# A transformer block on one core: half of the cross attention's output projection as a wide product, x^T scaled by ScalarE, finer first loads

## The chip, the core and the metric

The kernel runs on 1 core of a Trainium2 chip. The metric is the device time of one execution in microseconds; lower is better. The engines are called by their names or as the profile abbreviates them: TensorE (PE, its weight loads PEld), VectorE (DVE), ScalarE (ACT), GpSimd (POOL) and SyncE (SP), which issues most of the DMAs.

## What is computed

One layer of an encoder, batch 1, 256 tokens of 2048 features, all in f32, with weights from memory:

```
h  = rms_norm(x, g_mix);  proj = h @ w_in
x  = x + concat(MLA(proj), DiffAttention(proj)) @ w_out
hx, hm = rms_norm(x, g_xattn), rms_norm(mem, g_mem)
xq, xk, xv = hx @ w_xq, hm @ w_xk, hm @ w_xv          # 4 heads of 128, 256 memory tokens
xo = softmax(xq . xk / sqrt(128)) @ xv                 # 256 x 512
x  = x + xo @ w_xo                                     # 512 -> 2048
hf = rms_norm(x, g_ffn)
x  = x + (silu(hf @ w_gate) * (hf @ w_up)) @ w_down
out = rms_norm(x, g_final)
```

## The kernel before, in words

**Precision.** TensorE multiplies in a reduced f32 format, so each operand is split into a high part and a low part (names ending in `h` and `l`: `wh`, `wl` for weights, `x2T_h`, `x2T_l` for activations), and each product is three matmuls: high by high, high by low, low by high (`mm`, L99 to L101). The split (`split_into`) is a cast to the high part on ScalarE (L107) and a subtraction for the low part on VectorE (L108). Every weight that comes from memory goes through both engines once before TensorE can read it.

**Tiles.** The 256 tokens are two token tiles of 128 (`tt`). An output block is 128 tokens by 512 columns in one bank of PSUM. A K tile is 128 rows of the contraction. `project` runs over the K tiles of a 512-column block, with one accumulator for each token tile: 6 matmuls for a K tile.

**Wide products.** `wide_project` computes 1024 columns at once for both token tiles, over pairs of K tiles, so a pair is a 2 x 2 block product. A plain pair ("P") takes 8 block products, 24 matmuls. A summed pair ("W") computes the same with 7 block products, 21 matmuls, from sums and differences of blocks. Its activations need eight forms of 128 x 128 (`summed_pair`, L236 to L252): where they come from PSUM, ScalarE copies one block (`a21`, L244), VectorE makes four differences, each from the one before (L245 to L248), and then `split_into` makes high and low parts of the first four blocks and the four differences. Its weights need four sums on VectorE and their splits. The four products that are shared by two outputs stand in banks `q1`, `q5`, `q7`, `q6`, which are added into the residual stream `x_res` at the end (`leave`). Two groups of four PSUM banks change roles after each wide product (`banks.reverse()`).

**Order of work.** A scheduler places the instructions on each engine by simulated times, from the program text and the tile pools (24 buffers of activations, 3 of raw weights, 4 each of `wh` and `wl`). The loads of weights stay in program order on SP's queue. A buffer that isn't free, or an engine's order, is what an instruction waits for.

**The start.** The first projection (`w_in_lat`, 16 K tiles of 832 columns, 512 for the queries' and 320 for the keys' latents) begins as the first loads land. The x^T tiles (128 x 256 a K tile) are scaled by the gains (`gains`) and split in one go (`Transposed.load`): by ScalarE (L113), and for K tile 0 by VectorE (L111). Before, K tiles 0 and 1 are loaded singly, x^T and weights in turn; from K tile 2 on the weights come two K tiles at a time, x^T first two and then four. Two small tables for the positions (`pos`, `invf`) are queued behind the weights of K tiles 4 and 5; GpSimd and ScalarE make the trigonometric tables from them. Until the data are there, TensorE runs 12 matmuls of zeros (`wps`, L386).

**Around the change.** After the cross attention's heads (`heads_out`: value times transposed probabilities, into the bank `po`, two heads each, split into `xoT`), the output projection is four calls of `project` over 4 K tiles of `xoT`, one for each 512 columns. Each result is added to `x_res` by VectorE. Then `column_T` transposes the 512 new columns of a token tile with four TensorE transposes (L504) into a bank `pt`, VectorE multiplies them by the gains of the next norm into `x2T_f`, `split_into` makes `x2T_h` and `x2T_l`, and ScalarE takes the sum of squares (L206, `junk`). The gated feed-forward reads x2T: first a narrow chunk of 512 gate and 512 up columns (`project`, 16 K tiles), and then wide ones, for which `x2T_f` is multiplied by the row scale (`rrow`, L870) and split again as `x2n`.

```
x2T(kt):  K tiles 0-3 from column 0, 4-7 from column 1, 8-11 from column 2, 12-15 from column 3
```

## Time and profile before

| | |
|---|---|
| time, median of 3 runs | 1143.33 us (1143.21 to 1143.75) |
| the profiled execution | 1143.3 us, its span 1141.5 us |
| mean granted TensorE clock | 0.998 of full speed |
| TensorE busy | 1131.6 us, 99% of the span, 5394 matmuls and transposes recorded |
| VectorE busy | 980.6 us, 86% |
| ScalarE busy | 649.7 us, 57% |
| GpSimd busy | 57.6 us, 5% |
| DMA | 222.13 MB, mean 195 GB/s |

The span runs from the first to the last instruction of the profiled execution, and its time has what lies around it, 1.8 us. Times in the profile are counted from the span's start. A matmul's busy time reaches past the start of the next one, since they are pipelined; what a matmul costs is read from start to start.

### The profile page before, as it was taken

What the parts mean: (1) busy time and instruction counts of PE and PEld (TensorE: products, weight loads), DVE (VectorE), ACT (ScalarE), POOL (GpSimd) and SP (SyncE); (2) the same over time, 40 slices, a digit from 0 to 9 for tenths busy, and PEclk for the clock granted to TensorE, in tenths of its full rate; (3) what the DMA queues carried; (4) which work ended last, traced back from release to release, by engine and by line L of the source; (5) the groups of instructions that cost most, each with busy time, mean ns of one, the idle gap of its engine ahead of it and who ended that gap; (6) DMA issues with size and microseconds to landing.
All of it is one profiled execution on the core that took longest, in us unless ns stands there. A gap on an engine that the chain in (4) does not pass through costs nothing.

```text
span 1141.5 us, 14385 instructions
## 1 busy us (share of the span) xinstructions
PE 1131.6 (99%) x5394; PEld 946.4 (83%) x5394; DVE 980.6 (86%) x1341; ACT 649.7 (57%) x930; POOL 57.6 (5%) x75
## 2 busy tenths in 40 slices
PE   9999999999999999999999999999999999999997
PEld 7888888888888888888888888888888888888886
DVE  7688766878997776989899998998999898998975
ACT  6755455556567555665555464564554664654642
POOL 4920000000001000000000000000000000000000
PEclk9999999999999999999999999999999999999999
DMA  9655334536557445455655555555555555565543
GB/s 355 222 204 183 141 113 146 185 135 227 214 204 271 152 162 179 161 212 187 215 192 213 181 198 216 185 195 211 184 204 202 214 192 199 194 238 207 191 169 129
DMA packets 34485, 222.13 MB, mean 195 GB/s; under 512 B 4208, under 2 KB 4976, under 8 KB 10096
## 3 DMA queue, kind: packets, MB, share of 16 engines
q1 hardware_dynamic: 32688, 216.60, 53.3%
q0 software_dynamic: 864, 3.15, 0.8%
q10 hardware_dynamic: 864, 1.47, 0.4%
q8 instruction: 42, 0.69, 0.2%
q14 instruction: 27, 0.22, 0.1%
HBM read 219.11 MB, written 2.10 MB: 194 GB/s over the span
## 4 chain that ended last, share of the span: by engine, by line
PE 98%; DMA 1%; issue 0%; ACT 0%; DVE 0%; SPq 0%; POOLq 0%; POOL 0%; ACTq 0%
PE acc L100 26%; PE acc L99 26%; PE acc L101 26%; PE q L99 4%; PE q L100 4%; PE q L101 4%; PE pt L504 2%; PE ppt L652 1%; DMA wraw<-in_w_in_lat 1%; PE psc L100 1%; PE psc L101 1%; PE psc L99 1%; PE pt L924 0%; PE acckv L99 0%; PE acckv L101 0%
## 5 line engine op out<-in xcount | busy, mean ns | idle before, releaser
L107 ACT CAST wh<-wraw 128x1024 fp32r<-128x1024 f32 (+2 forms) x401 | 389.3, 990 | 331.7 <-PE acc L101 285.5
L108 DVE TENSOR_TENSOR wl<-wraw,wh 128x1024 fp32r<-128x1024 f32 (+2 forms) x401 | 455.3, 1150 | 91.0 <-ACT wh L107 89.6
L107 ACT CAST wh<-tsum 128x1024 fp32r<-128x1024 f32 (+1 forms) x96 | 96.4, 1006 | 52.7 <-PE acc L101 23.1
L100 PE MATMUL acc<-wl,x2n_h 128*128 128x512 f32 x320 | 124.5, 390 | 0.0
L101 PE MATMUL acc<-wh,x2n_l 128*128 128x512 f32 x320 | 123.9, 389 | 0.0
L108 DVE TENSOR_TENSOR wl<-tsum,wh 128x1024 fp32r<-128x1024 f32 (+1 forms) x96 | 111.5, 1163 | 14.1 <-ACT wh L107 14.0
L99 PE MATMUL acc<-wh,x2n_h 128*128 128x512 f32 x320 | 109.7, 390 | 0.0
L100 PE MATMUL acc<-wl,x0T_h 128*128 128x512 f32 x224 | 88.7, 396 | 0.1
L101 PE MATMUL acc<-wh,x0T_l 128*128 128x512 f32 x224 | 88.2, 394 | 0.0
L99 PE MATMUL acc<-wh,x0T_h 128*128 128x512 f32 x224 | 86.8, 395 | 0.7 <-ACT wh L107 0.5
L100 PE MATMUL acc<-wl,hT_h 128*128 128x512 f32 x188 | 73.3, 392 | 0.0
L100 PE MATMUL q<-wl,forms_h 128*128 128x512 f32 x187 | 72.7, 389 | 0.0
L101 PE MATMUL q<-wh,forms_l 128*128 128x512 f32 x187 | 72.6, 389 | 0.0
L101 PE MATMUL acc<-wh,hT_l 128*128 128x512 f32 x188 | 72.4, 389 | 0.0
L101 PEld LDWEIGHTS acc<-wh,x2n_l 128*128 128x128 f32 x320 | 60.1, 188 | 12.4
L100 PEld LDWEIGHTS acc<-wl,x2n_h 128*128 128x128 f32 x320 | 60.1, 188 | 12.3
L99 PEld LDWEIGHTS acc<-wh,x2n_h 128*128 128x128 f32 x320 | 59.9, 188 | 12.3
L99 PE MATMUL q<-wh,forms_h 128*128 128x512 f32 x187 | 65.6, 389 | 0.0
L100 PE MATMUL acc<-wl,forms_h 128*128 128x512 f32 x167 | 64.8, 389 | 0.0
L101 PE MATMUL acc<-wh,forms_l 128*128 128x512 f32 x167 | 64.8, 389 | 0.0
L99 PE MATMUL acc<-wh,hT_h 128*128 128x512 f32 x188 | 64.5, 391 | 0.0
L99 PE MATMUL acc<-wh,forms_h 128*128 128x512 f32 x167 | 62.9, 389 | 0.0
(406 smaller groups left out, 2240.4 us busy)
## 6 DMA issues: line engine op xcount, KB each, us to landing
wraw<-in_w_gate SPq DMA_DIRECT2D x44, 1024.0 KB, 4.8
wraw<-in_w_up SPq DMA_DIRECT2D x44, 1024.0 KB, 4.8
wraw<-in_w_dn SPq DMA_DIRECT2D x41, 1024.0 KB, 4.8
wraw<-in_w_in SPq DMA_DIRECT2D x24, 1024.0 KB, 4.8
wraw<-in_w_out SPq DMA_DIRECT2D x16, 1024.0 KB, 4.9
wraw<-in_w_in_lat SPq DMA_DIRECT2D x7, 832.0 KB, 7.5
wraw<-in_w_xk SPq DMA_DIRECT2D x4, 1024.0 KB, 4.9
wraw<-in_w_xq SPq DMA_DIRECT2D x4, 1024.0 KB, 5.0
```

Source lines behind the costliest of these rows:

```text
L99: nc.tensor.matmul(o, l.h, r.h, start=start, stop=False)
L100: nc.tensor.matmul(o, l.h, r.l, start=False, stop=False)
L101: nc.tensor.matmul(o, l.l, r.h, start=False, stop=stop)
L107: last_cast[0] = nc.scalar.copy(out=dst.h, in_=src).ins
L108: last_split[0] = nc.vector.tensor_tensor(out=dst.l, in0=src, in1=dst.h.bitcast(F32), op=ALU.subtract).ins
L504: nc.tensor.transpose(out=pt[:, j * P:(j + 1) * P], in_=src[:, j * P:(j + 1) * P], identity=ident)
L652: nc.tensor.transpose(out=pt[:, kt * S + tt * P:kt * S + (tt + 1) * P], in_=p[:, tt, kt * P:(kt + 1) * P], identity=ident)
```

## The change

It has four parts. **(1)** The first 1024 columns of the cross attention's output become one `wide_add` over two pairs of K tiles: the first pair (heads 0 and 1) is summed, the second plain. `heads_out` makes the summed pair's forms straight from the bank `po`, so these heads exist as forms only, and the remaining two `project` calls take their K tiles from the pair's first forms. As the summed pair is the first to write three of the accumulators, the start flags are taken from `used`. **(2)** In `transposed`, the gain is applied to the x2T columns by four ScalarE passes, one for each 128 columns, with the gain as the scale of the pass. **(3)** K tiles 0 to 5 of the start are loaded singly, x^T and weights in turn, and x^T comes two K tiles at a time from there on. **(4)** The warm-up has three matmuls of 256 columns in place of four. The host packs `w_xo` to match.

```diff
+XO_KINDS = "WP"
...
             mm(Q[1], A11, b11[:, 0, :], *own)
-            mm(accs[0][1], S3, b11[:, 1, :], False, stop)
+            mm(accs[0][1], S3, b11[:, 1, :], not used[0][1], stop)
             mm(Q[5], S5, t1, *own)
             mm(Q[7], S7, t3, *own)
-            mm(accs[0][0], A12, b21[:, 0, :], False, stop)
+            mm(accs[0][0], A12, b21[:, 0, :], not used[0][0], stop)
             mm(Q[6], S6, t2, *own)
-            mm(accs[1][0], A22, t4, False, stop)
+            mm(accs[1][0], A22, t4, not used[1][0], stop)
+            for tt, oc in ((0, 1), (0, 0), (1, 0)):
+                used[tt][oc] = True
...
-    for n in [512] * 8 + [256] * 4:
+    for n in [512] * 8 + [256] * 3:
         nc.tensor.matmul(wps[:, :n], warm[:, :P], warm[:, :n], start=True, stop=True)
...
-        def load_one(self, k):
-            self.load(0, k, 1)
+        def load_one(self, kt):
+            self.load(kt // 4, kt % 4, 1)
...
     for i in range(8):
-        if i == 1:
-            x0T.load(0, 2, 2)
-        elif i and i % 2 == 0:
-            x0T.load(i // 2)
+        one_by_one = i < 3
+        if not one_by_one:
+            x0T.load(i // 2, i % 2 * 2, 2)
...
-        for k, w in enumerate(weights(a["w_in_lat"][i], i == 0, before_k=x0T.load_one if i == 0 else None,
+        for k, w in enumerate(weights(a["w_in_lat"][i], one_by_one,
+                                      before_k=lambda k: one_by_one and x0T.load_one(2 * i + k),
                                       cut=QL if i == 0 else None, raw=lat_raw if i == 0 else None)):
...
-    def transposed(dst, src, tt, n, gain=None, raw=None):
+    def transposed(dst, src, tt, n, gain=None, raw=None, by_scalar=False):
...
-            nc.vector.tensor_tensor(out=g[:, :n, :], in0=pv, in1=gain.unsqueeze(2).to_broadcast([P, n, P]),
-                                    op=ALU.mult)
+            if by_scalar:
+                for j in range(n):
+                    nc.scalar.activation(g[:, j, :], pv[:, j, :], AF.Copy, scale=gain[:, j:j + 1])
+            else:
+                nc.vector.tensor_tensor(out=g[:, :n, :], in0=pv, in1=gain.unsqueeze(2).to_broadcast([P, n, P]),
+                                        op=ALU.mult)
...
-        split_into(dst, po.rearrange("p (j t) -> p j t", j=2))
+        po = po.rearrange("p (j t) -> p j t", j=2)
+        if dst is None:
+            return summed_pair(po[:, :, :P], po[:, :, P:], True)
+        split_into(dst, po)
+        return Pair(dst)
...
-        transposed(t, xs, tt, 4, gain[:, 4 * oc:4 * oc + 4], raw)
+        transposed(t, xs, tt, 4, gain[:, 4 * oc:4 * oc + 4], raw, raw is not None)
...
-    xoT = act_tile(name="xoT")
-    for half in range(2):
-        heads_out(xoT[:, 2 * half:2 * half + 2, :], [pxT[half][:, 0:2, :], pxT[half][:, 2:4, :]], xv, 2 * half)
+    xoT = act_tile(name="xoT")[:, 0:2, :]
+    xo = [heads_out([None, xoT][half], [pxT[half][:, 0:2, :], pxT[half][:, 2:4, :]], xv, 2 * half)
+          for half in range(2)]
...
+    wide_add(xo, a["w_xo2"], (0, 1), XO_KINDS, 0)
     for oc in range(4):
-        accs = project(lambda kt: xoT[:, kt, :], [a["w_xo"][oc, 0]])
+        if oc >= 2:
+            add_out(project(lambda kt: tuple(xo[kt // 2].at(kt % 2, tt) for tt in range(NT)), [a["w_xo"][oc - 2, 0]]), oc)
         x2p.append(act_tile(name="x2T"))
         x2raw.append(act.tile([P, 4, S], F32, name="x2T_f", tag="act"))
         for tt in range(NT):
-            xs = x_res[tt][:, oc * 512:(oc + 1) * 512]
-            nc.vector.tensor_tensor(out=xs, in0=xs, in1=accs[tt], op=ALU.add)
             column_T(x2p[oc], oc, tt, g_f, x2ss, x2raw[oc])
```

The change adds two or more lines above every line of the program, so L99 to L101 become L101 to L103, L107 and L108 become L109 and L110, L206 becomes L208, L504 becomes L508, L870 becomes L882; the ScalarE passes with the gain are L514. Numbers behind a name are the tile's.

TensorE, from the last value product of the second half of the heads into the output projection; before:

```order
L101 MATMUL po_4071<-pxT_h_3808,val_l_4049 128x256
L99 MATMUL po_4071<-pxT_h_3808,val_h_4048 128x256
L100 MATMUL po_4071<-pxT_l_3809,val_h_4048 128x256
L101 MATMUL po_4071<-pxT_h_3808,val_l_4049 128x256
L99 MATMUL acc_4087<-wh_4091,xoT_h_4054 128x512
L100 MATMUL acc_4087<-wl_4092,xoT_h_4054 128x512
L99 MATMUL acc_4088<-wh_4091,xoT_h_4054 128x512
L100 MATMUL acc_4088<-wl_4092,xoT_h_4054 128x512
```

and with the change:

```order
L103 MATMUL po_4095<-pxT_h_3819,val_l_4060 128x256
L101 MATMUL po_4095<-pxT_h_3819,val_h_4059 128x256
L102 MATMUL po_4095<-pxT_l_3820,val_h_4059 128x256
L103 MATMUL po_4095<-pxT_h_3819,val_l_4060 128x256
L101 MATMUL q1_4117<-wh_4121,forms_h_4080 128x512
L102 MATMUL q1_4117<-wl_4122,forms_h_4080 128x512
L103 MATMUL q1_4117<-wh_4121,forms_l_4081 128x512
L101 MATMUL acc_4112<-wh_4121,forms_h_4080 128x512
L102 MATMUL acc_4112<-wl_4122,forms_h_4080 128x512
L101 MATMUL q5_4118<-wh_4134,forms_h_4080 128x512
L102 MATMUL q5_4118<-wl_4135,forms_h_4080 128x512
L101 MATMUL acc_4111<-wh_4125,forms_h_4080 128x512
```

The last four rows before the projection are the same. Before, its first matmul reads the high part of heads 0 and 1 (xoT_h), which takes one cast; now it reads the first pair's forms, and the seven matmuls behind it read them too.

TensorE, from the end of the last output projection to the gate, with the change (pt_4239 is token tile 1 of column 0, pt_4255 and pt_4268 are column 1, pt_4322 and pt_4335 column 2, pt_4389 and pt_4402 column 3; acc_4427 and acc_4428 are the gate's accumulators for the two token tiles):

```order
L103 MATMUL acc_4349<-wh_4356,xoT_l_4066 128x512
L508 MATMUL pt_4239<-ident_104,xres1_112 128x128 x4
L508 MATMUL pt_4255<-ident_104,xres0_111 128x128 x4
L508 MATMUL pt_4268<-ident_104,xres1_112 128x128 x4
L508 MATMUL pt_4322<-ident_104,xres0_111 128x128 x4
L101 MATMUL acc_4427<-wh_4431,x2T_h_4223 128x512
L102 MATMUL acc_4427<-wl_4432,x2T_h_4223 128x512
L103 MATMUL acc_4427<-wh_4431,x2T_l_4224 128x512
L101 MATMUL acc_4427<-wh_4431,x2T_h_4223 128x512
L102 MATMUL acc_4427<-wl_4432,x2T_h_4223 128x512
L103 MATMUL acc_4427<-wh_4431,x2T_l_4224 128x512
L101 MATMUL acc_4427<-wh_4435,x2T_h_4223 128x512
```

and a little further, behind pt_4335's four transposes and five more gate matmuls:

```order
L508 MATMUL pt_4389<-ident_104,xres0_111 128x128 x4
L508 MATMUL pt_4402<-ident_104,xres1_112 128x128 x4
L101 MATMUL acc_4428<-wh_4431,x2T_h_4223 128x512
L102 MATMUL acc_4428<-wl_4432,x2T_h_4223 128x512
L101 MATMUL acc_4427<-wh_4465,x2T_h_4252 128x512
```

The transposes of column 0's second token tile now stand behind the whole last product, and twelve more of them, twelve gate matmuls and another twelve transposes stand between them and the first matmul of acc_4428.

ScalarE in the same place; before:

```order
L206 ACTIVATE junk_4196,x2ss_4086<-xres0_112 128x512
L206 ACTIVATE junk_4207,x2ss_4086<-xres1_113 128x512
L107 CAST x2T_h_4123<-x2T_f_4125 128x4x128
L107 CAST wh_4347<-wraw_4345 128x1024
L107 CAST x2T_h_4123<-x2T_f_4125 128x4x128
L107 CAST x2T_h_4184<-x2T_f_4186 128x4x128
L107 CAST wh_4351<-wraw_4345 128x1024
L107 CAST x2T_h_4184<-x2T_f_4186 128x4x128
L206 ACTIVATE junk_4257,x2ss_4086<-xres0_112 128x512
L107 CAST wh_4381<-wraw_4379 128x1024
```

and with the change:

```order
L109 CAST wh_4431<-wraw_4429 128x1024
L109 CAST wh_4435<-wraw_4429 128x1024
L208 ACTIVATE junk_4346,x2ss_4110<-xres1_112 128x512
L514 ACTIVATE x2T_f_4225<-pt_4239,gains_101 128x128 x4
L514 ACTIVATE x2T_f_4254<-pt_4255,gains_101 128x128 x4
L514 ACTIVATE x2T_f_4254<-pt_4268,gains_101 128x128 x4
L208 ACTIVATE junk_4400,x2ss_4110<-xres0_111 128x512
L109 CAST wh_4465<-wraw_4463 128x1024
L109 CAST wh_4469<-wraw_4463 128x1024
L109 CAST x2T_h_4223<-x2T_f_4225 128x4x128
L109 CAST x2T_h_4252<-x2T_f_4254 128x4x128 x2
```

Before, the casts of column 0's two token tiles (x2T_h_4123) stand with one weight cast between them. Now the first one's stands further ahead, and between the second one's transposes (pt_4239) and its cast (x2T_h_4223) stand twelve scaled passes, two sums of squares and two weight casts.

VectorE, at the end of the narrow gate's weights and the row scale; before:

```order
L108 TENSOR_TENSOR wl_4454<-wraw_4447,wh_4453 128x1024
L108 TENSOR_TENSOR wl_4553<-wraw_4550,wh_4552 128x1024
L108 TENSOR_TENSOR wl_4557<-wraw_4550,wh_4556 128x1024
L108 TENSOR_TENSOR wl_4587<-wraw_4584,wh_4586 128x1024
L108 TENSOR_TENSOR wl_4591<-wraw_4584,wh_4590 128x1024
L870 TENSOR_TENSOR x2T_f_4125<-x2T_f_4125,rrow_4487 128x1024
L870 TENSOR_TENSOR x2T_f_4186<-x2T_f_4186,rrow_4487 128x1024
L870 TENSOR_TENSOR x2T_f_4247<-x2T_f_4247,rrow_4487 128x1024
L870 TENSOR_TENSOR x2T_f_4308<-x2T_f_4308,rrow_4487 128x1024
L108 TENSOR_TENSOR wl_4621<-wraw_4618,wh_4620 128x1024
```

and with the change:

```order
L110 TENSOR_TENSOR wl_4534<-wraw_4531,wh_4533 128x1024
L110 TENSOR_TENSOR x2T_l_4387<-x2T_f_4388,x2T_h_4386 128x4x128 x2
L110 TENSOR_TENSOR wl_4538<-wraw_4531,wh_4537 128x1024
L882 TENSOR_TENSOR x2T_f_4225<-x2T_f_4225,rrow_4571 128x1024
L882 TENSOR_TENSOR x2T_f_4254<-x2T_f_4254,rrow_4571 128x1024
L882 TENSOR_TENSOR x2T_f_4321<-x2T_f_4321,rrow_4571 128x1024
L882 TENSOR_TENSOR x2T_f_4388<-x2T_f_4388,rrow_4571 128x1024
L110 TENSOR_TENSOR wl_4637<-wraw_4634,wh_4636 128x1024
L110 TENSOR_TENSOR wl_4641<-wraw_4634,wh_4640 128x1024
```

The four multiplications by the row scale stood behind the splits of four weight tiles of the up product (wl_4553 to wl_4591); now they stand ahead of them.

## Rows read from the trace of the kernel before

**Rows 1.** Page, chain of work that ended last: share of the span by engine.
```profile
PE 98%; DMA 1%; issue 0%; ACT 0%; DVE 0%; SPq 0%; POOLq 0%; POOL 0%; ACTq 0%
```

**Rows 2.** Timeline, 0 to 45 us: start, busy us, what ran [idle before <-releaser].
```profile
4.54 0.35 DVE L111 TENSOR_SCALAR x0T_h<-xraw,gains 128x256 fp32r<-128x256 f32 x1 [3.42 <-DMA gains<-in_gains]
...
10.11 0.31 PE L101 MATMUL acckv<-wh,x0T_l 128*128 128x320 f32 x1
...
10.93 0.50 PE L99 MATMUL acc<-wh,x0T_h 128*128 128x512 f32 x1 [0.51 <-ACT wh L107]
...
11.64 0.31 PE L99 MATMUL acckv<-wh,x0T_h 128*128 128x320 f32 x1
...
11.98 0.50 PE L100 MATMUL acc<-wl,x0T_h 128*128 128x512 f32 x1
```

**Rows 3.** Timeline, ScalarE, 0 to 40 us; and DMA GB/s, one number per us.
```profile
7.22 0.98 ACT L107 CAST wh<-wraw 128x512 fp32r<-128x512 f32 x2 [1.61 <-DMA wraw<-in_w_in_lat]
...
9.99 1.68 ACT L107 CAST wh<-wraw 128x832 fp32r<-128x832 f32 x2 [0.97 <-DMA wraw<-in_w_in_lat]
...
GB/s 0 16 194 370 299 332 383 399 376 419 435 358 144 300 428 409 435 432 399 426 406 461 397 393 417 437 413 436 417 407 430 437 387 148 213 393 418 41 57 221
```

**Rows 4.** Timeline, VectorE from 53 us and TensorE from 56 us.
```profile
53.57 1.05 DVE L520 TENSOR_SCALAR cq<-cq,rq 128x512 f32<-128x512 f32 x2 [3.32 <-POOL rq L200]
...
54.53 1.27 DVE L108 TENSOR_TENSOR wl<-wraw,wh 128x1024 fp32r<-128x1024 f32 x1
...
56.20 0.39 PE L100 MATMUL acc<-wl,x0T_h 128*128 128x512 f32 x1
...
56.88 0.39 PE L100 MATMUL acc<-wl,x0T_h 128*128 128x512 f32 x1
```

**Rows 5.** Timeline, TensorE and ScalarE, end of the cross-attention heads, 402 to 412 us.
```profile
407.25 0.28 PE L100 MATMUL po<-pxT_l,val_h 128*128 128x256 f32 x1
...
408.33 0.50 PE L99 MATMUL acc<-wh,xoT_h 128*128 128x512 f32 x1
...
407.69 0.59 ACT L107 CAST xoT_h<-po 128x512 fp32r<-128x512 f32 x1 [1.14 <-PE po L101]
```

**Rows 6.** Timeline, ScalarE and VectorE, forms of an earlier summed pair, 259.5 to 267 us.
```profile
261.20 0.27 ACT L244 COPY a<-pdt 128x128 f32<-128x128 f32 x1
...
262.83 0.37 ACT L107 CAST forms_h<-pdt 128x256 fp32r<-128x256 f32 x1 [1.36 <-DVE sums L248]
...
261.80 0.28 DVE L245 TENSOR_TENSOR sums<-a,pdt 128x128 f32<-128x128 f32 x1
...
262.52 0.28 DVE L248 TENSOR_TENSOR sums<-pdt,sums 128x128 f32<-128x128 f32 x1
```

**Rows 7.** Timeline, ScalarE: its passes of several kinds, 0 to 75 us.
```profile
53.49 0.29 ACT L549 ACTIVATE sind<-turns 128x128 f32<-128x128 f32 x1
...
54.29 1.99 ACT L107 CAST wh<-wraw 128x1024 fp32r<-128x1024 f32 x2
...
11.57 1.70 ACT L113 ACTIVATE x0T_h<-xraw,gains 128x256 fp32r<-128x256 f32 x4
...
27.01 0.63 ACT L206 ACTIVATE junk<-xres 128x512 bf16<-128x512 f32 x1
...
27.77 0.63 ACT L206 ACTIVATE junk<-xres 128x512 bf16<-128x512 f32 x1
```

**Rows 8.** Timeline, TensorE: transposes, 58 to 74 us.
```profile
59.38 1.04 PE L504 MATMUL pt<-ident,cq 128*128 128x128 f32 x8
```

**Rows 9.** Timeline, VectorE: row scale of x^T and what follows, 432 to 470 us.
```profile
458.22 4.62 DVE L870 TENSOR_TENSOR x2T_f<-x2T_f,rrow 128x1024 f32<-128x1024 f32 x4
...
462.76 1.22 DVE L108 TENSOR_TENSOR wl<-wraw,wh 128x1024 fp32r<-128x1024 f32 x1
...
463.90 0.68 DVE L108 TENSOR_TENSOR x2n_l<-x2T_f,x2n_h 128x512 fp32r<-128x512 f32 x1
...
467.59 1.22 DVE L108 TENSOR_TENSOR wl<-wraw,wh 128x1024 fp32r<-128x1024 f32 x1
```

More of the change, by code (lines that the diff above doesn't have):

```diff
@@ L1064, in _lay_out @@
         "w_xv": _pieces(i["w_xv"][0])[0],
-        "w_xo": _pieces(i["w_xo"][0]),
+        "w_xo2": _pairs(i["w_xo"][0][:, :1024], XO_KINDS)[0],
+        "w_xo": _pieces(i["w_xo"][0][:, 1024:]),
         "w_gate0": _pieces(i["w_gate"][0][:, :512]),
```

## The prediction, made before the changed kernel ran

> **What bounds the kernel now.** I read the chain of waits first: TensorE holds 98% of it [rows 1]. So an edit counts only by what it takes from TensorE's own stream or by a wait that it makes or ends there. The timeline then gives the price of TensorE's work: matmuls of 512 columns start 0.227 us apart (three from 56.20 to 56.88) [rows 4], transposes 0.11 apart (eight in 1.04) [rows 8], and it stands still almost nowhere after 12 us. The sum is made against the profiled execution, 1143.3 us (span 1141.5), the same as the median of the runs, 1143.33.
>
> **Output projection: matmuls.** Before, 4 column blocks take 96 matmuls; now the summed pair takes 21, the plain pair 24, the other two blocks 48: 93. Three fewer: 3 x 0.227 = **-0.7 us**.
>
> **The summed pair's forms.** Before, the first product needs one cast of the finished heads: ScalarE starts it at 407.69, and TensorE goes on at 408.33 without a gap, because the second half's products cover it [rows 5]. Now (first order piece) TensorE's next matmul reads forms_h. Those are made by a chain: ScalarE's copy (a21), four VectorE operations on its result, and only then the casts. The same chain stands in the trace before the earlier wide product: copy at 261.20, 0.27 long; VectorE's four from 261.80 to 262.80; first cast at 262.83, 0.37 long [rows 6]. There VectorE was busy until 261.79; here it is free by then, so its first operation follows the copy by some 0.06. Put at 407.69: 0.27 + 0.06 + 1.00 + 0.03 + 0.37 = 1.73, done at 409.42, against 408.33 wanted: a new wait of 1.1. Nothing else stands in TensorE's order to fill it. Ends 0.8 and 1.5, I take **+1.1**. The later forms come in time: the cast of the sums ends 0.5 later, and three matmuls stand ahead of its first reader. Loads for the pair (two adds and casts more for weights) lie ahead of 407 and beside xv's products; the casts that a plain pair needs start as soon as the first forms' products free their buffers.
>
> **Columns 0 and 1, scaled by ScalarE.** This moves 8 VectorE passes to 32 ScalarE passes of 128 columns. The price of one is not in the trace: four passes of 128 columns with a constant scale take 0.80 (53.49 to 54.29), 0.20 each; passes of 256 columns with a scale per partition 0.40 each (four in 1.70, the last 0.5 long) [rows 7]. I take 0.27: the columns are those of the first, the scale operand that of the second. VectorE is busy in this stretch, but no TensorE wait came of it, so its relief is worth 0 by itself.
>
> What it costs is in the second and third order piece. Count from the moment TensorE has ended the four transposes of column 0's second token tile (z = 0; they now stand behind the whole last product). Until it needs that tile's cast (x2T_h, first matmul into the second accumulator of the gate) TensorE has 12 transposes, 12 matmuls and 12 transposes: 1.3 + 2.7 + 1.3 = 5.3. ScalarE in the same time has, in its order: 0.2 latency and 0.2 of a weight cast, one square sum 0.76, 12 scaled passes 3.2, one square sum 0.76, two weight casts 1.9 (0.94 each), and then the cast, 0.6: 7.6 [rows 7]. TensorE waits **2.2**; with passes of 0.20 or 0.40 it is 1.4 or 3.8. Right behind it the low part: VectorE must first do two weight splits of 1.14 that wait for those two casts, so x2T_l is there at about 9.0, wanted at 8.5: **+0.5** (ends 0.2 and 0.8). Before, both token tiles came with one cast each behind single weight casts, and VectorE's pass ran beside.
>
> **Behind the gate.** ScalarE's queue runs late on: from that cast to the last gate weights it has 16 more scaled passes 4.3, seven casts of 512 or 1024 columns for x and four for weights, some 12 us in all, so the last gate split ends near z = 20.8. In the fourth order piece VectorE does the four multiplications by the row scale (4.62 [rows 9]) ahead of the up weights' splits; before, they stood behind four of them. So 20.8 + 4.6 + two splits 2.3 + sixteen small operations 5.7 (eleven such take 3.7, 463.90 to 467.59) + the third split 1.2 [rows 9] = 34.6. TensorE restarts at z = 7.6 and gets there after 36 matmuls, 0.5 of wait, two transposes and 74 matmuls: 33.3. A wait of 1.3; at the end of so long a sum I count **+1.0** (ends 0 and 1.9).
>
> **The start.** Of 16 K tiles the third is late: TensorE stands from 10.11 + 0.15 to 10.93, and again from 11.64 + 0.15 to 11.98, 0.67 + 0.20 beyond its pace [rows 2], waiting for the cast of a load of two K tiles that arrived at 9.99 [rows 3]. Loads land in the order of issue, some 1.3 us behind the bytes: by the bytes per microsecond, 1152 KB (up to the second K tile) had passed at 5.8 and its cast began at 7.22; 2266 KB (up to the late load) at 8.7, cast 9.99 [rows 3]. Loaded singly, the third tile ends at 1709 KB: passed at 7.3, there at 8.6, cast by 9.5, before TensorE asks at 10.26. Both stalls go: **-0.9** (end 0). The two small tables behind those loads come behind the same bytes as before (3.64 MB), so GpSimd's chain from them starts as before. The trigonometric chain sets VectorE free at 53.57, after 3.32 of idle behind GpSimd; its split ends at 55.80 and TensorE reads it at 56.88 [rows 4]: 1.08 of slack, of which the gain uses 0.87. The cover just holds. One warm-up matmul less is worth 0: the first real one waits for VectorE's first pass at 4.54, and that for the gains' transfer [rows 2].
>
> Many smaller transfers: with pieces of 128 to 832 KB in flight the queue moves 300 to 435 KB a microsecond from 5 to 11 us [rows 3], so I put no price on the split. The Trainium skill (DMA: Bandwidth & Descriptors, Rules for kernel authors) asks for transfers of 1 MiB or more; its table would, as an estimate from that page, bring a K tile's 0.56 MB in 1.6 us at best and 4 us at its 64 KB rate, which would eat the gain, so the sum would be 0.9 higher. This trace, with its 300 to 435, speaks against that here.
>
> **Sum.** 1143.3 - 0.7 - 0.9 + 1.1 + 2.2 + 0.5 + 1.0 = **1146.5 us**. All low ends (0.8, 1.4, 0.2, 0) give 1144.1; all high ends with no gain at the start (1.5, 3.8, 0.8, 1.9, -0.7) give 1150.6. Between, 1144.6 to 1148.4 is its own range.
>
> **Rivals.**
> *The relief pays (not slower).* VectorE was the crowded engine behind the projection and ScalarE had gaps there. If ScalarE's passes run in those gaps and nothing of the gate waits, only the forms' wait is left: 1143.3 - 0.7 - 0.9 + 1.1 = 1142.8. It decides by the time ScalarE needs for the twelve passes and three other casts between the transposes and x2T_h: under 5.3 us in all, that is if a scaled pass cost under 0.1. For it: TensorE never waited for ScalarE here before. Against it: even the shortest row, 0.20 a pass, leaves 1.4 of wait, and the order piece puts 12 passes ahead. The Trainium skill (Perfetto Trace Analysis, Optimizing Scalar/DVE Operations) says that work moved to ScalarE may pay where VectorE is saturated, and that breaking an operation up lets some work end sooner; by that rule this rival is the outcome. Chance 0.34, as my durations of a pass are borrowed and the order could be met with slack that I don't see.
> *The start's gain is lost.* GpSimd's tables come later than before, since their issue now stands behind more small ones; over 0.2 us more and the split at 55.80 is late for TensorE: 1146.5 + 0.9 = 1147.4. For it: slack of 1.08 against 0.87. Against it: the same bytes ahead. Chance 0.06.
> *Everything covered (faster).* No wait at the forms either, and the losses round the heads (about 0.5) gone too: 1143.3 - 1.6 - 0.5 = 1141.2, or beyond. It needs casts ready before their inputs. Chance 0.08, as the order of everything behind the projection has moved too.
> Forecast: chance 0.52.
>
> **How the numbers follow.** 0.2% of 1143.3 is 2.3 us, about what a measurement of this kernel tells from no change. Slower by more (over 1145.6): five sixths of the forecast and the whole second rival, 0.43 + 0.06 = 0.49. Faster by more (under 1141.0): most of the fully covered case, which lies near that bound, 0.06. The rest, 0.45, is within. The range 1142.3 to 1148.4 takes in the first rival and the forecast's own range, and leaves out the far ends, the fully covered case and a part of each tail.
>
> **What would show it.** In the changed kernel's profile: 93 projection matmuls; before the first matmul that reads forms_h an idle TensorE of about 1.1, ended by ScalarE's forms_h; before the second accumulator's first gate matmul about 2, ended by x2T_h; 16 us later a short one ended by a weight split; at the start no gap at the third K tile, and TensorE about 0.9 ahead at 15 us. I am wrong if scaled passes stand much closer than 0.2 apart, if the gate's matmuls follow each other without a gap, or if the tables' arrival moves GpSimd's chain.

## The result, and the profile after

| | before | with the change |
|---|---|---|
| median | 1143.3 us (1142.66 to 1143.79, 14 runs) | 1145.63 us (1145.18 to 1146.83, 14 runs) |
| the profiled execution | 1143.3, span 1141.5 | 1146.83, span 1145.0 |

The ratio is 1.0021, 95% interval 1.0014 to 1.0029: 2.3 us slower, inside the range given, 0.9 below the forecast. The profiled execution is the slowest of its 14, 1.2 above their median. A second profile of the same kernel (run e5 below), of 1145.54 us, is nearer to the median, and the two are read side by side.

The chain of work that ended last, from the page, was 98% TensorE [rows 1] and is now:

```profile
PE 95%; DVE 2%; ACT 1%; issue 1%; DMA 0%; SPq 0%; POOLq 0%; POOL 0%; ACTq 0%
```

VectorE and ScalarE have come onto it. What TensorE waited for between 400 and 480 us (the view of waits: line, releaser, us in total, times, longest) in the kernel before:

```profile
PE po L99 <- ACT val_h L113: 0.2, 1, 0.2
```

and with the change:

```profile
PE acc L101 <- ACT x2T_h L109: 1.4, 1, 1.4
PE q L101 <- ACT forms_h L109: 1.0, 1, 1.0
PE acc L103 <- DVE x2T_l L110: 0.3, 1, 0.3
```

Three new waits in an otherwise closed stream. They are the three that the prediction placed: forms, x2T_h, x2T_l.

**The forms.** The timeline of the changed kernel, ScalarE and VectorE and TensorE at the end of the heads (start, busy us, what ran, idle before and releaser), to set beside [rows 5, 6]:

```profile
407.04 0.27 ACT L246 COPY a<-po 128x128 f32<-128x128 f32 x1 [1.57 <-PE po L103]
407.34 0.29 DVE L247 TENSOR_TENSOR sums<-a,po 128x128 f32<-128x128 f32 x1 [0.96 <-ACT a L246]
...
408.06 0.28 DVE L250 TENSOR_TENSOR sums<-po,sums 128x128 f32<-128x128 f32 x1
408.38 0.37 ACT L109 CAST forms_h<-po 128x256 fp32r<-128x256 f32 x1 [1.07 <-DVE sums L250]
...
407.56 0.28 PE L103 MATMUL po<-pxT_h,val_l 128*128 128x256 f32 x1
408.80 0.50 PE L101 MATMUL q<-wh,forms_h 128*128 128x512 f32 x1 [0.97 <-ACT forms_h L109]
```

The copy, four differences and a cast take 407.04 to 408.75. The last value product starts at 407.56, and the next matmul 1.24 behind it in place of 0.12: 1.12 lost.

**The gate.** The same view 23 us later, ScalarE's queue, VectorE's, and TensorE:

```profile
429.35 1.98 ACT L109 CAST wh<-wraw 128x1024 fp32r<-128x1024 f32 x2
431.24 0.63 ACT L208 ACTIVATE junk<-xres 128x512 bf16<-128x512 f32 x1
...
431.86 3.19 ACT L514 ACTIVATE x2T_f<-pt,gains 128x128 f32<-128x128 f32 x12
434.87 0.70 ACT L208 ACTIVATE junk<-xres 128x512 bf16<-128x512 f32 x1
...
435.48 2.06 ACT L109 CAST wh<-wraw 128x1024 fp32r<-128x1024 f32 x2
437.36 1.73 ACT L109 CAST x2T_h<-x2T_f 128x512 fp32r<-128x512 f32 x3
...
436.62 2.36 DVE L110 TENSOR_TENSOR wl<-wraw,wh 128x1024 fp32r<-128x1024 f32 x2 [2.96 <-ACT wh L109]
438.90 1.89 DVE L110 TENSOR_TENSOR x2T_l<-x2T_f,x2T_h 128x512 fp32r<-128x512 f32 x3
...
430.51 1.91 PE L508 MATMUL pt<-ident,xres 128*128 128x128 f32 x16
435.68 1.03 PE L508 MATMUL pt<-ident,xres 128*128 128x128 f32 x8
438.11 0.50 PE L101 MATMUL acc<-wh,x2T_h 128*128 128x512 f32 x1 [1.40 <-ACT x2T_h L109]
438.96 0.40 PE L102 MATMUL acc<-wl,x2T_h 128*128 128x512 f32 x1
439.64 0.72 PE L103 MATMUL acc<-wh,x2T_l 128*128 128x512 f32 x1 [0.28 <-DVE x2T_l L110]
```

ScalarE is busy from 429.35 to 443.75 without a pause. Twelve scaled passes take 3.19, 0.27 each as estimated (0.25 from start to start, as the next instruction begins at 434.87). The cast that TensorE waits for begins at 437.36, behind everything that was counted ahead of it, and TensorE loses 1.56 beyond its pace (its last transpose starts at 436.44, the next matmul at 438.11, against 0.11) and then 0.45 (438.96 to 439.64, against 0.23).

**TensorE's clock.** The view by stretches (us, then busy time and count of PE, PEld, DVE, ACT, POOL; PEclk, DMA share, GB/s), first profile of the changed kernel:

```profile
431.00:439.00 8.00, 6.60 (x41) 5.24 (x39) 5.04 (x6) 8.00 (x23) 0.00 (x0) 1.00 0.34 131
439.00:440.00 1.00, 0.72 (x3) 0.36 (x2) 1.00 (x2) 1.00 (x5) 0.00 (x0) 0.88 0.04 8
440.00:443.00 3.00, 3.00 (x8) 2.32 (x8) 2.07 (x7) 3.00 (x9) 0.69 (x1) 0.50 0.87 322
```

Behind the two waits the granted clock stands at 0.50, its lower level of 1.2 GHz, for 3 us: matmuls start 0.427 apart in place of 0.227. From 439.64 nine starts take 3.76 (to 443.40) where the second profile takes 2.16 (439.18 to 441.34), so 1.6 us go. In the second profile the same two waits stand at 437.65 and 439.18, and the granted clock is 1.00 throughout:

```profile
437.65 0.50 PE L101 MATMUL acc<-wh,x2T_h 128*128 128x512 f32 x1 [1.40 <-ACT x2T_h L109]
439.18 0.50 PE L103 MATMUL acc<-wh,x2T_l 128*128 128x512 f32 x1 [0.29 <-DVE x2T_l L110]
```

```profile
431.00:444.00 13.00, 11.31 (x58) 8.83 (x57) 8.88 (x14) 13.00 (x35) 0.69 (x1) 1.00 0.46 163
```

So the lower clock came behind these waits once in two profiles. How many of the 14 runs had it is not known: the four longest (1145.92 to 1146.83) have a mean granted clock of 0.998 and the other ten 0.999, but the second profile has 0.998 too, without the low stretch.

**Behind the gate.** In the second profile a third wait stands 26 us later, at 463.4. In the first it is 0.2 only; there TensorE comes to the place at 465.5, 2.1 us later, and the split it needs begins only 1.3 later (464.63). VectorE and TensorE in the second profile:

```profile
450.76 4.62 DVE L882 TENSOR_TENSOR x2T_f<-x2T_f,rrow 128x1024 f32<-128x1024 f32 x4
455.30 2.35 DVE L110 TENSOR_TENSOR wl<-wraw,wh 128x1024 fp32r<-128x1024 f32 x2
...
463.34 2.35 DVE L110 TENSOR_TENSOR wl<-wraw,wh 128x1024 fp32r<-128x1024 f32 x2
...
463.15 0.61 PE L101 MATMUL acc<-wh,x2T_h 128*128 128x512 f32 x2
464.61 0.50 PE L102 MATMUL acc<-wl,x2T_h 128*128 128x512 f32 x1 [0.85 <-DVE wl L110]
```

The row scale, two splits, the small operations, and then the third split of the up weights: TensorE loses 1.01.

**The start.** TensorE in the first 11 us (first profile), beside [rows 2]:

```profile
8.34 0.73 PE L101 MATMUL acc<-wh,x0T_h 128*128 128x512 f32 x2 [0.22 <-ACT wh L109]
...
10.71 0.39 PE L101 MATMUL acc<-wh,x0T_h 128*128 128x512 f32 x1
```

The gap ahead of the third K tile (10.71) is gone; one of 0.22 ahead of the second is new. At 35 us TensorE is 0.6 ahead of the kernel before in the first profile and 1.1 in the second.

### The profile page after: what moved, and what is told of

Its sections match the earlier page's. It is cut to its first block, busy times and chain, and to the rows that moved or that the text cites. A ratio compares the mean times of both kernels' runs of the same rounds, so it can differ in the third digit from the quotient of the medians.

```text
span 1145.0 us, 14454 instructions
## 1 busy us (share of the span) xinstructions
PE 1133.4 (99%) x5390; PEld 947.6 (83%) x5390; DVE 986.9 (86%) x1355; ACT 660.7 (58%) x970; POOL 56.4 (5%) x75
## 4 chain that ended last, share of the span: by engine, by line
PE 95%; DVE 2%; ACT 1%; issue 1%; DMA 0%; SPq 0%; POOLq 0%; POOL 0%; ACTq 0%
PE acc L103 25%; PE acc L102 25%; PE acc L101 25%; PE q L101 4%; PE q L102 4%; PE q L103 4%; PE pt L508 1%; DVE wl L110 1%; PE ppt L660 1%; PE psc L103 1%; PE psc L102 1%; PE psc L101 1%; DMA wraw<-in_w_in_lat 0%; DVE x2T_f L882 0%; ACT wh L109 0%
## 5 line engine op out<-in xcount | busy, mean ns | idle before, releaser
L109 ACT CAST wh<-wraw 128x1024 fp32r<-128x1024 f32 (+2 forms) x401 | 389.0, 990 | 322.6 <-PE acc L103 270.3
L110 DVE TENSOR_TENSOR wl<-wraw,wh 128x1024 fp32r<-128x1024 f32 (+2 forms) x401 | 454.2, 1148 | 85.7 <-ACT wh L109 84.4
L109 ACT CAST wh<-tsum 128x1024 fp32r<-128x1024 f32 (+1 forms) x98 | 97.6, 998 | 52.9 <-PE acc L103 24.0
L110 DVE TENSOR_TENSOR wl<-tsum,wh 128x1024 fp32r<-128x1024 f32 (+1 forms) x98 | 112.9, 1154 | 13.3 <-ACT wh L109 13.0
L103 PE MATMUL acc<-wh,x2n_l 128*128 128x512 f32 x320 | 124.0, 389 | 0.0
L101 PE MATMUL acc<-wh,x2n_h 128*128 128x512 f32 x320 | 109.2, 390 | 0.0
L103 PE MATMUL acc<-wh,x0T_l 128*128 128x512 f32 x224 | 88.2, 394 | 0.0
L101 PE MATMUL acc<-wh,x0T_h 128*128 128x512 f32 x224 | 87.2, 397 | 0.2 <-ACT wh L109 0.2
L103 PE MATMUL q<-wh,forms_l 128*128 128x512 f32 x190 | 73.8, 389 | 0.0
L103 PE MATMUL acc<-wh,hT_l 128*128 128x512 f32 x188 | 72.4, 389 | 0.0
L103 PEld LDWEIGHTS acc<-wh,x2n_l 128*128 128x128 f32 x320 | 60.1, 188 | 12.3
L101 PEld LDWEIGHTS acc<-wh,x2n_h 128*128 128x128 f32 x320 | 59.9, 188 | 12.3
L102 PE MATMUL acc<-wl,forms_h 128*128 128x512 f32 x177 | 68.7, 389 | 0.0
L103 PE MATMUL acc<-wh,forms_l 128*128 128x512 f32 x177 | 68.4, 389 | 0.0
L101 PE MATMUL q<-wh,forms_h 128*128 128x512 f32 x190 | 67.2, 390 | 1.0 <-ACT forms_h L109 1.0
L101 PE MATMUL acc<-wh,forms_h 128*128 128x512 f32 x177 | 66.6, 389 | 0.0
L101 PE MATMUL acc<-wh,hT_h 128*128 128x512 f32 x188 | 64.9, 391 | 0.0
```

The lines of the kernel that those rows point to most:

```text
L101: nc.tensor.matmul(o, l.h, r.h, start=start, stop=False)
L102: nc.tensor.matmul(o, l.h, r.l, start=False, stop=False)
L103: nc.tensor.matmul(o, l.l, r.h, start=False, stop=stop)
L109: last_cast[0] = nc.scalar.copy(out=dst.h, in_=src).ins
L110: last_split[0] = nc.vector.tensor_tensor(out=dst.l, in0=src, in1=dst.h.bitcast(F32), op=ALU.subtract).ins
```

## The experiments

The theory was the prediction's: the wide product makes one wait for its forms; the scaled passes, queued on ScalarE ahead of x2T_h, make the one at the gate and the clock's fall behind it. The rivals: that the place of the transposes makes the gate's wait, whoever scales; that the passes cost wherever they stand; that the start's gain is lost again. The changes here are a few tenths of a per cent, so the interval beside each ratio says whether it is told from no change. All times are medians; the ratio is to the kernel before, run on the same chip (1143.08 for e1 to e4, 1143.18 for e5 to e8, 1143.40 for e9 and e10).

| run | what | us | ratio (95%) |
|---|---|---|---|
| e1 | change, scaling by VectorE | 1143.15 | 0.9999 (0.9991 to 1.0008) |
| e2 | before + start | 1142.17 | 0.9992 (0.9983 to 1.0001) |
| e3 | before + scaling by ScalarE | 1143.27 | 1.0000 (0.9991 to 1.0009) |
| e4 | wide product on the last half | 1149.65 | 1.0057 (1.0043 to 1.0071) |
| e5 | change, second profile | 1145.54 | one run |
| e6 | change, casts ahead of passes | 1144.98 | 1.0014 (1.0005 to 1.0022) |
| e7 | e2 with four warm-up matmuls | 1142.07 | 0.9990 (0.9981 to 0.9999) |
| e8 | e2 with four K tiles singly | 1142.25 | 0.9992 (0.9983 to 1.0001) |
| e9 | e1, x2T_l ahead of two splits | 1142.17 | 0.9989 (0.9980 to 0.9998) |
| e10 | e1, forms cast first | 1144.64 | 1.0011 (1.0002 to 1.0020) |

### e1: the scaling back on VectorE

```diff
-        transposed(t, xs, tt, 4, gain[:, 4 * oc:4 * oc + 4], raw, raw is not None)
+        transposed(t, xs, tt, 4, gain[:, 4 * oc:4 * oc + 4], raw)
```

> The change with x2T's gain scaling back on VectorE; wide product, loads and warm-up as in the change. TensorE's order is the same as the changed kernel's, so column 0's second token tile is still transposed behind the whole last product. Theory (the queue of scaled passes on ScalarE makes the gate wait): the wait of 1.40 ahead of the gate's second accumulator falls under 0.5, TensorE's clock stays at its upper level there, the wait for the forms stays at 1.1; 1143.3 - 0.65 - 0.68 + 1.1 + 0.3 = 1143.4 us (1143.0 to 1144.2). Rival (the place of the transposes makes it, and VectorE, crowded with the adds of the wide product, is as late as ScalarE): a wait of 1 to 2 stays, ended by x2T_h or x2T_l, and the time stays at 1145.0 or above.

1143.15, inside the range. Against its own kernel before, e1 costs 0.1 and the change 2.3; the two medians differ by 2.5. So 2.3 to 2.5 us of the change's time go with the passes. TensorE and VectorE at the gate:

```profile
435.58 0.48 PE L101 MATMUL acc<-wh,x2T_h 128*128 128x512 f32 x1
...
437.60 0.50 PE L103 MATMUL acc<-wh,x2T_l 128*128 128x512 f32 x1 [0.85 <-DVE x2T_l L110]
...
434.60 2.35 DVE L110 TENSOR_TENSOR wl<-wraw,wh 128x1024 fp32r<-128x1024 f32 x2
436.87 1.28 DVE L110 TENSOR_TENSOR x2T_l<-x2T_f,x2T_h 128x512 fp32r<-128x512 f32 x2
```

Nothing waits for x2T_h any more and the clock stays at 1.00, as the theory has it. But 1.01 is lost at x2T_l (436.36 to 437.60), where under 0.5 was expected: the rival was half right, as VectorE is late in its turn.

### e2, e7, e8: the start alone

e2 is the kernel before with the change's hunks on `load_one`, the loop over `i` and the warm-up alone. e7 and e8 change one number of it:

```diff
-    for n in [512] * 8 + [256] * 3:
+    for n in [512] * 8 + [256] * 4:        # e7
...
-        one_by_one = i < 3
+        one_by_one = i < 2                 # e8
```

> The kernel before with only the start of the change: six K tiles loaded singly, x^T two at a time behind, one warm-up matmul less. Theory: TensorE is 0.6 to 0.7 earlier from 15 us on and keeps it to the end: 1142.65 us (1142.4 to 1142.9). Rival (the gain is lost at the trigonometric tables, which come no sooner): 1143.3, with a new wait of about 0.6 near 56 us.

> The kernel before with the finer loads of the start, but all four warm-up matmuls of 256 columns. Theory (the first real matmul waits for VectorE's first pass or starts as the warm-up ends, whichever is later): no difference to the start with three beyond 0.1 or 0.2: 1142.2 us (1142.0 to 1142.5). Rival (the missing warm-up matmul is part of the gain): 1142.5 or above, with the first real matmul 0.2 later.

> The kernel before with four K tiles of the start loaded singly in place of six, x^T two at a time behind, three warm-up matmuls. Theory (it was the load of K tiles 2 and 3 in one that came late): the same gain as with six, 1142.2 us (1142.0 to 1142.6). Rival (the wait goes to the next load of two K tiles): a gap of 0.3 or more ahead of K tile 4, 1142.6 to 1143.1.

1142.17, 1142.07 and 1142.25, against 1143.08 and 1143.18: the finer loads give 0.9 to 1.1. The interval of e7 is clear of no change, those of e2 and e8 just reach it (1.0001), and the three agree. For e2 1142.4 to 1142.9 was expected, from the first profile's 0.65, and the gain was larger. It is kept to the end: in e2's profile TensorE is 0.8 ahead of the kernel before at the first transposes (59 us) and at its last matmul. The fourth warm-up matmul does nothing either way. In e8 no gap comes ahead of K tile 4; its profile has one of 0.50 ahead of K tile 1, where the change's has one of 0.22, and the median is the same. So of the new single loads it is those of K tiles 2 and 3 that pay.

### e3: the scaled passes alone

The kernel before with the hunks on `transposed` and `column_T` alone.

> The kernel before with only the scaling moved to ScalarE: 32 passes of 0.27, the output projection and the loads as before. In this order columns 0 and 1 are transposed inside the projection's matmuls, as before. Theory (the passes cost only because the wide product leaves column 0's transposes behind it): gate wait under 0.5, 1143.3 to 1143.9 us. Rival (8.6 us of passes on ScalarE are too much wherever they stand): a wait of 1 or more ended by x2T_h or a weight cast, 1144.5 us or more.

1143.27 against 1143.08: nothing. TensorE waits nowhere at the gate, and ScalarE is as crowded as in the change, but from 420 us on (the view by stretches):

```profile
420.00:440.00 20.00, 20.00 (x103) 16.55 (x102) 14.79 (x22) 19.53 (x55) 0.69 (x1) 1.00 0.55 200
```

ACT is the fourth busy time. Columns 0 and 1 are transposed inside the projection there (from 418.9 to 425.3, its last matmul at 431.8), so their passes have its matmuls as cover. In the change 28 of the 32 transposes stand behind the projection's last matmul, and of the two kernels only that one pays for the passes.

### e6: the same instructions, casts ahead of passes

```diff
         for tt in range(NT):
-            column_T(x2p[oc], oc, tt, g_f, x2ss, x2raw[oc])
+            with tc.issue_after(last_cast[0]):
+                column_T(x2p[oc], oc, tt, g_f, x2ss, x2raw[oc])
```

> The changed kernel with one order more: on ScalarE, the passes of each token tile of x2T stand behind the cast of the token tile before it, so column 0's second cast has 4 passes and two weight casts ahead of it in place of 12 passes, two sums of squares and two weight casts. The same instructions, none less. Theory (the queue ahead of that one cast makes the gate wait): ScalarE needs 1.07 + 1.9 + 0.6 = 3.6 from the transposes and TensorE asks 4.7 behind them, so no wait at the gate's second accumulator, and the clock stays up; the wait for forms stays at 1.0; 1142.6 us (1142.2 to 1143.3). Rival (ScalarE has too much to do there, in whichever order): the wait comes back at column 1 or at a gate weight, 1 us or more, 1144.3 or above.

1144.98, not the 1142.2 to 1143.3 of the theory: the rival was right. The new condition holds for the transposes too, so eight of them move behind the gate's second accumulator, and TensorE asks for its cast sooner. Even so nothing waits there, so the queue ahead of that cast did make that wait. But the lateness comes back, with TensorE's two waits and ScalarE's stretches:

```profile
448.44 0.50 PE L103 MATMUL acc<-wh,x2T_l 128*128 128x512 f32 x1 [0.41 <-DVE x2T_l L110]
...
474.86 0.50 PE L102 MATMUL acc<-wl,x2T_h 128*128 128x512 f32 x1 [1.06 <-DVE wl L110]
```

```profile
431.00:440.00 9.00, 9.00 (x50) 7.47 (x49) 5.99 (x7) 9.00 (x25) 0.00 (x0) 1.00 0.60 229
440.00:450.00 10.00, 9.59 (x45) 7.54 (x44) 6.86 (x8) 10.00 (x27) 0.00 (x0) 1.00 0.32 110
```

ScalarE is busy for all of 19 us, where before it was for 11.1 of the 20 from 430 to 450. Its casts feed VectorE's splits, and those come late at column 2 and at the up weights.

### e5: the change once more

> The changed kernel once more, for a second profile. Theory: the waits come back where they were, 1.0 for forms_h and about 1.9 in all at the gate for x2T_h and x2T_l, within 0.2 each. Open is the stretch of halved TensorE clock behind the gate's wait (granted 0.50 from 440 to 443 us in the first profile, about 1.5 us lost): if it follows from the wait it is there again; if it was chance the second profile has none, and the time is near 1145.2 us in place of 1146.8.

The waits came back within 0.02 (1.12 at the forms, 1.56 and 0.45 at the gate), the lower clock did not, and the 1.01 behind the gate showed. 1145.54 us: what the clock does not take the later wait does, in part.

### e9: the same for VectorE

```diff
-            for w in weights(src, i < fine):
+            if hold is not None and i == 1:
+                with tc.issue_after(hold):
+                    ws = weights(src)
+            else:
+                ws = weights(src, i < fine)
+            for w in ws:
...
-        ga = project(x2T, [a["w_gate0"][0, i] for i in range(4)])
+        ga = project(x2T, [a["w_gate0"][0, i] for i in range(4)], hold=x2_split)
```

(`x2_split` is the last split of column 0.)

> As the version with VectorE's scaling (wide product and start as in the change), with one order more: on VectorE the splits of the gate's second weight piece stand behind the low part of column 0's x2T in place of ahead of it. The same instructions. Theory (the 1.0 left at the gate there is VectorE doing two weight splits of 1.15 ahead of x2T_l): that wait falls under 0.2, the wait for forms stays at 1.0, 1143.15 - 1.0 = 1142.2 us (1141.9 to 1142.6). Rival (VectorE has too much to do in the stretch, so the wait only moves, as it did on ScalarE): a wait of 0.5 or more at a gate weight of the next piece or later, 1142.8 or more.

1142.17, as forecast: the wait at x2T_l (now at 436.92) is gone and none takes its place. VectorE had room; it had only the wrong order. The wait for forms stands as it was:

```profile
407.38 0.28 PE L103 MATMUL po<-pxT_h,val_l 128*128 128x256 f32 x1
408.62 0.50 PE L101 MATMUL q<-wh,forms_h 128*128 128x512 f32 x1 [0.97 <-ACT forms_h L109]
...
436.45 0.40 PE L102 MATMUL acc<-wl,x2T_h 128*128 128x512 f32 x1
...
436.92 0.39 PE L103 MATMUL acc<-wh,x2T_l 128*128 128x512 f32 x1
```

e9 has the wide product and the start, e2 the start alone, and both take 1142.17, on two chips (0.9989 and 0.9992 of the kernel before). In their profiles both are 0.77 ahead at the first transposes, and at the last matmul e9 is 0.61 and e2 0.79 ahead. So of the three matmuls saved (0.7) the wait for forms (1.1) leaves nothing.

### e10: the forms cast first

In `summed_pair`, for the heads' pair, the blocks of the bank are split ahead of the copy and the differences; in `wide_project` the products with A11, A12 and A22 come first; columns 1 to 3 are transposed from within the gate's loop.

```diff
+        if forms_first:
+            split_into(f[:, 0:2, :], a0)
+            split_into(f[:, 2:4, :], a1)
         a21 = a1[:, 0, :]
...
+            if kinds is XO_KINDS:
+                mm(accs[0][0], A12, b21[:, 0, :], not used[0][0], stop)
+                mm(accs[1][0], A22, t4, not used[1][0], stop)
             mm(accs[0][1], S3, b11[:, 1, :], not used[0][1], stop)
```

> As the version with VectorE's scaling, with the forms that need no difference cast first: ScalarE casts the four blocks of the bank before it copies one for the differences, the summed pair's products that read only those four come first, and columns 1 to 3 are transposed behind the gate's weight splits of the piece before. Theory (the wait for forms is the chain of a copy and four differences ahead of the first cast): the wait ahead of the first matmul that reads forms_h falls from 1.0 under 0.2. By the lengths in the first trace, the plain pair's weights then come late by 0.7 to 1.0, as their buffers and ScalarE are free only at 408.3, so most of it is given back there; the gate waits 0.5 or less: 1142.3 us (1141.4 to 1142.9). Rival (the first cast waits for something else, the bank itself or ScalarE): the wait ahead of forms_h stays at 0.8 or more.

1144.64, above the range of 1141.4 to 1142.9. The wait ahead of forms_h is gone, so the chain of copy and differences was its cause. TensorE:

```profile
407.00 0.28 PE L103 MATMUL po<-pxT_h,val_l 128*128 128x256 f32 x1
407.12 0.40 PE L101 MATMUL q<-wh,forms_h 128*128 128x512 f32 x1
...
409.85 0.73 PE L101 MATMUL acc<-wh,xoT_h 128*128 128x512 f32 x2 [0.34 <-ACT wh L109]
411.11 0.50 PE L102 MATMUL acc<-wl,xoT_h 128*128 128x512 f32 x1 [0.52 <-DVE wl L110]
...
413.15 0.50 PE L101 MATMUL acc<-wh,forms_h 128*128 128x512 f32 x1 [0.84 <-ACT forms_h L109]
```

In its place come the plain pair's weights, 0.61 and 0.69 late, and then the forms of the differences, 1.01 late, since ScalarE copies their block only behind the weight cast. The expected give-back of 0.7 to 1.0 was 2.3. The waits for forms (1.12) and at x2T_l (1.01) that e1 has are both gone, so these lines make e10 0.2 slower than e1; by the medians, each against its own kernel before, it is 1.2. No run shows where the rest goes.

### e4: the wide product on the last half

Columns 0 and 1 by `project`, columns 2 and 3 by the wide product, its summed pair (now heads 2 and 3) first; their transposes behind the gate's first pieces; VectorE scales.

```diff
+    for oc in range(2):
+        add_out(project(lambda kt: tuple(xo[kt // 2].at(kt % 2, tt) for tt in range(NT)), [a["w_xo"][oc, 0]]), oc)
+        x2_column(oc)
+    wide_add(xo, a["w_xo2"], (1, 0), XO_KINDS, 2)
...
+            with tc.issue_after(last_mm[0]), tc.issue_after(last_cast[0]), tc.issue_after(last_split[0]):
+                x2_column(late_columns[i])
```

> A version meant to keep the three matmuls less and both waits out: columns 0 and 1 of the output by the plain projection, the wide product for columns 2 and 3 with the second pair summed and done first, their transposes put behind the gate's first K tiles, the scaling on VectorE, the start as in the change. Theory: the first matmul behind the heads reads the plain pair, so no wait for forms beyond that of before, and no wait at the gate: 1143.3 - 0.65 - 0.68 = 1142.0 us (1141.7 to 1142.6). Rival (VectorE's nine operations and four adds of the wide product stand ahead of the gate's weight splits, and TensorE waits for wl): a wait of 2 or more at the gate's first matmuls, 1144 us or more.

1149.65, where 1141.7 to 1142.6 was expected: the rival, and more. VectorE and TensorE at the gate, and the clock behind:

```profile
428.63 0.69 DVE L362 TENSOR_TENSOR v<-q,u 128x512 f32<-128x512 f32 x1 [0.23 <-PE q L103]
...
433.56 1.87 DVE L372 TENSOR_TENSOR xres<-xres,acc 128x512 f32<-128x512 f32 x3
435.35 4.62 DVE L110 TENSOR_TENSOR wl<-wraw,wh 128x1024 fp32r<-128x1024 f32 x4
...
436.62 0.80 PE L102 MATMUL acc<-wl,x2T_h 128*128 128x512 f32 x1 [4.86 <-DVE wl L110]
```

```profile
436.00:442.00 6.00, 5.38 (x13) 4.22 (x14) 4.58 (x8) 3.59 (x7) 0.69 (x1) 0.50 0.54 184
```

The operations that take the wide product's banks apart stand from 428.63 to 435.35 ahead of the gate's first split. TensorE waits 4.86, and its clock is at the lower level for the 6 us behind. Another 0.9 goes at the heads, where VectorE has the low part of the values (`val_l`) late.

## Why the prediction held, point by point

| term | forecast | first profile | second profile | by a run of its own |
|---|---|---|---|---|
| three matmuls | -0.7 | -0.7 | -0.7 | |
| forms | +1.1 | +1.12 | +1.12 | gone in e10 |
| x2T_h at the gate | +2.2 | +1.56 | +1.56 | gone in e1, e6 |
| x2T_l behind it | +0.5 | +0.45 | +0.45 | gone in e6, e9 |
| up weights | +1.0 | +0.2 | +1.01 | |
| start | -0.9 | -0.6 | -1.1 | -0.9 to -1.1 (e2, e7, e8) |
| lower clock | none | +1.6 | 0 | |

The -0.7 is counted (93 matmuls in place of 96), not measured by itself. Both profiles lose 0.2 more at the gate's first weight split. With it the columns make +3.8 and +2.5, and TensorE's last matmul starts 3.9 and 2.6 later than in the kernel before. The spans are only 3.5 and 2.2 longer, as 7.3 us lie behind that matmul in place of 7.8. Why is not known: e3, with the old start, has 7.8 too, and the runs with the new start have 7.3 to 7.6. The medians differ by 2.3.

That the first profile's 1146.83 lies so near to the 1146.5 of the forecast is luck: the clock's 1.6, which no term had, stands in for the 0.6 and 0.8 by which the gate and the up weights came out smaller.

**Mis-sized: the gate.** The step "7.6 against 5.3" was 7.0 against 5.6. The transposes of column 0's second tile end at 430.94 (430.51 and four of 0.11). TensorE asks at 436.55, 5.6 later, and x2T_h is there at 437.97, 7.0 later. ScalarE's instructions took less than I had counted: a square sum 0.62 from its start to the next instruction's (431.24 to 431.86) in place of 0.76, the twelve passes 3.0 (431.86 to 434.87) in place of 3.2. TensorE took 0.3 more, at the gate's first two matmuls (432.17 to 432.92, 0.75 in place of 0.45).

**A slip.** The signs named a short wait "16 us later". By the sum's own numbers (33.3 less 7.6) it is 26 us behind the gate's wait, and there it stood.

**Left out: the clock.** The sum let TensorE go on at full pace behind each wait. In one of two profiles of this kernel it did not, and lost 1.6 us. Not all of that stays in the time: where TensorE is late already, the next wait is shorter (0.2 in place of 1.01).

**The reason was narrower than the truth.** The prediction blamed the passes ahead of one cast. e3 shows that the passes are free where the projection covers them, and e6 that moving them behind that cast only moves the lateness on: ScalarE is full for 19 us, as seven of the eight token tiles are transposed behind the projection. It takes both parts of the change together: the passes without the wide product cost 0.2, no more than noise (e3), the wide product and the start without the passes 0.1 (e1), all together 2.3. That VectorE's relief is worth nothing was right in the kernel before; in the changed order it is not quite so, as e1 loses 1.01 at x2T_l, though that is VectorE's order, as e9 shows, and not its load.

**The rivals.** "The relief pays" is out: the version without it (e1) is 2.3 to 2.5 faster. There the Trainium skill (Perfetto Trace Analysis, Optimizing Scalar/DVE Operations) spoke for the change; its condition, a saturated VectorE, was not met, as VectorE was busy for 15.3 of 20 us from 430 to 450 in the kernel before. "The start's gain is lost" is out by e2. "Everything covered" is out by the 1.12 at the forms, in both profiles of the change. For the many smaller transfers the trace decided against the estimate drawn from the Trainium skill (DMA: Bandwidth & Descriptors, Rules for kernel authors): 0.9 to 1.1 gained, none eaten.

The fastest versions found are the start alone, 1142.07 to 1142.25 in e2, e7 and e8, and e9, 1142.17: about 1.0 below the kernel before and 3.5 below the change.

## What to carry to other kernels

Ahead of a moved piece of work, count the whole queue of the engine that gets it, up to the next thing that the bound engine asks for; the same 32 passes (8.6 us of ScalarE) cost 0.2 where the projection's matmuls covered half of them and over 2 where nearly all transposes came at its end. A product with fewer matmuls pays only if the chain that makes its operands has other matmuls to hide behind: here three matmuls were to buy 0.7, and the chain took 1.1. A reordering that removes a wait tells order from load: on VectorE the wait was gone for good (e9), on ScalarE it came back 10 and 37 us later (e6).

## What was not expected of the hardware

The lower clock came behind the same pair of waits in one execution and not in the other, and behind 4.86 us of idleness in e4.

At the start, the same instructions run at different paces in different executions. The warm-up matmuls start 0.427 apart at first, the pace that the trace shows at a granted clock of 0.50 behind the gate. The pace of 0.23 begins at about 3.9 us in the kernel before and at about 6.3 in the changed kernel's first profile. The view by stretches prints 1.00 from 0 us on in both, but it prints 1.00 also where the trace has no entry for the clock, and the entries begin at 3.93 and 6.26 us. In all twelve profiles the pace changes within some tenths of a us of the first entry (3.93 to 6.77 us). So, by their pace, the matmuls ahead of it run at the lower level of 1.2 GHz, and a 1.00 there tells nothing.

The start itself differs between profiles: at the first transposes (59 us) the eight with the change's start are 0.6 to 1.3 ahead of the kernel before, and e3, which has the old start, 0.5. So only medians tell what a change there is worth. The clock's first entry does not explain all of it: e3 has it later than the kernel before (5.07) and is ahead.
